# Projecting gates, fox values and memory values 512 columns at a time with four token sums open

## The chip, the cores and the metric

The kernel runs on one core of a Trainium2 chip. The metric is the device time of one execution in microseconds (us); lower is better. A core has a matrix engine (TensorE, "PE" in the profile, with its weight loads listed as PEld), VectorE (DVE), ScalarE (ACT), GpSimd (POOL) and SyncE (SP), which issues most of the transfers. Matrix products accumulate in PSUM, eight banks of 512 float32 columns by 128 partitions.

## What is computed

One layer of a streaming-encoder trunk over 512 tokens of width 1024, in float32:

```python
hn = rmsnorm(h, norm_mix_g[l])
fq, fk, fv, ff, gq, gf, gi, gg = jnp.split(hn @ w_in[l], split_idx, axis=-1)
fox_out = fox_attention(heads(fq), heads(fk), heads(fv), log_f)      # 8 heads of 64, causal, forget bias
rec = hgrn2_chunkwise(gq, gf, gi, lbs[l])                            # 4 heads, gated linear recurrence
rec = rmsnorm(rec, hgrn_norm_g[l]) * silu(gg)
h = h + concat([fox_out, rec]) @ w_out[l]
h = h + memory_cross_attention(rmsnorm(h, norm_x_g[l]), rmsnorm(mem, ...), w_xq[l], w_xkv[l], w_xo[l])
h = h + square(relu(rmsnorm(h, norm_ff_g[l]) @ w1[l])) @ w2[l]
return rmsnorm(h, final_norm_g)
```

Three of these products matter here: the output gates `gg` (512 tokens x 512 columns), the fox values `fv` (512 x 512) and the memory values, the second half of `mem_n @ w_xkv` (256 memory rows x 1024 columns, called xv in the kernel). Each has an inner dimension of 1024.

## The kernel before

**Products.** Every operand is split in two parts, hi (the value rounded to the format float32r) and lo (what the rounding left), and a product is made of three matmuls: hi x hi, hi x lo, lo x hi. The inner dimension is cut into 8 slices of 128 rows. `gemm_fm` makes a block with features on the partitions: 128 weight columns are the stationary operand and 512 tokens move. `gemm_tm` (lines 232 to 243) makes a block with tokens on the partitions: 128 tokens of the activations are stationary and the weight columns move, 256 at a time. The gates, the recurrence's inputs, the fox values and the memory values are made by `gemm_tm`. Two token tiles of 256 columns share one PSUM bank (`proj_tm`, line 547).

**Weights.** `specs` (line 132) lists the weight panels in the order of their use; a panel is 1024 rows by 256 columns. `load_unit` fetches half of it (four row slices, 512 KB) through SyncE's queue into one of two raw buffers; ScalarE then writes the hi part and VectorE the lo part into one of four buffers each. `next_panel` hands out the next panel and keeps one more panel loading ahead.

**PSUM.** The pools are mm (three banks), pv (one), sc (two) and tr (two).

**Order of the work.** The order on TensorE is the order in the code; the other engines' instructions are ordered by a planner by priority. Between the steps of the recurrence and of the fox attention, which wait for VectorE and ScalarE, the code lets TensorE work on projections from a queue called `fill` (class `Fill`, line 249). Each projection is a generator that gives back, after each three matmuls, its cost as a credit: 3n/2400 for n moving columns. `fill.run(us)` adds a credit and takes steps from the queue's head until the credit is used up; `fill.until(name)` takes steps until the named projection is finished, whatever the credit. In order the queue holds: proj_if and gi; the two gate panels (demanded before line 714); proj0, which makes the first pair of fox heads' queries and keys (`fox_proj`); fv0, the first 256 fox value columns; in the fox loop (line 909) proj1 mixed with the transposes of the memory, xv0; proj2, fv256; proj3, xv1 to xv3, and the four memory key panels xk0 to xk3.

**Fox loop.** It runs over 32 units: four pairs of heads, four token blocks, two heads. Unit n's scores are made, then 1.4 of filler (A1), then the output of the block finished three units ago (`fox_out`), then 0.8 of filler (A2), then the transposes of unit n-1's probabilities. At n = 2 the first fox values are demanded (line 931). After the loop what is left of the filler is run, the residual is fetched back (`load_hT`) and the output projection w_out begins (`wo`), whose columns read slices 4 to 7 of the mixed activations (the recurrence) before slices 0 to 3 (the four fox pairs).

**Slots.** Twelve s4 slots of 4 KB per partition hold the recurrence's tensors, the fox values, the memory and its transposes, the memory values and later the residual.

**Lines touched.** 132 to 147 (panels), 172 to 201 (loading), 547 to 583 (gates), 722 to 727 and 895 (fox values), 816 to 827 (memory values), 912 to 931 (the fox loop's demands).

Of the kernel before, what the change touches and what calls it, by code (L numbers as in the profile page):

```python
# [9 lines left out]
F32 = mybir.dt.float32  # L10
R = mybir.dt.float32r
U8 = mybir.dt.uint8
AF = mybir.ActivationFunctionType
# [18 lines left out]
GF = 5  # L32
WARM = 6
P1, P2, P3, P4, PW = 20, 20, 20, 10, -20
MT, NF, V0, LAG = 3, 2, 1, 3
F1, F2, F3, F4, B1 = 1.6, 2.7, 1.5, 1.0, 2.0
A1, A2 = 1.4, 0.8
X1, X2, X3, X4 = 1.5, 2.0, 1.5, 2.0
# [4 lines left out]
def emit(  # L43
# [49 lines left out]
    def s4(shape, name, dt=F32):  # L93
        return s4p.tile([P] + shape, dt, tag="s4", name=name)
# [18 lines left out]
    def mm(name, shape=(S,)):  # L113
        return mmp.tile([P] + list(shape), F32, tag="mm", name=name)

    def pvt(name):
        return pvp.tile([P, S], F32, tag="pv", name=name)
# [7 lines left out]
    def f(a):  # L125
        return a.bitcast(F32)


    def panel(w, n0):
        return [(slice(0, WT), w[:, n0 : n0 + WT].rearrange("(k p) n -> p k n", p=P))]  # L130

    specs = []
    for n0 in (2056, 2312, 1544, 1800, 2568, 2824, 3080, 3336):
        specs.append(panel(w_in, n0))
    specs[4].append((slice(WT, WT + FH), w_in[:, 1536:1544].rearrange("(k p) n -> p k n", p=P)))
    def pair(p):
        return [
            (slice(0, P), w_in[:, p * P : (p + 1) * P].rearrange("(k p) n -> p k n", p=P)),
            (slice(P, 2 * P), w_in[:, 512 + p * P : 512 + (p + 1) * P].rearrange("(k p) n -> p k n", p=P)),
        ]  # L140

    xv = [panel(w_xkv, D + j * WT) for j in range(4)]
    specs += [pair(0), panel(w_in, 1024), pair(1), *xv[0:V0], pair(2), panel(w_in, 1024 + WT), pair(3), *xv[V0:]]
    for j in range(4):
        specs.append(panel(w_xkv, j * WT))
    for w in (w_out, w_xq, w_xo):
# [10 lines left out]
    def new_parts(shape, name):  # L157
        pad = [P, UK * (UW + FH)]
        hi = whp.tile([P, shape[0] * shape[1]], R, tag="wh", name=f"wh{name}", padded_shape=pad)
        lo = wlp.tile([P, shape[0] * shape[1]], R, tag="wl", name=f"wl{name}", padded_shape=pad)  # L160
        return [t.rearrange("p (k n) -> p k n", k=shape[0]) for t in (hi, lo)]
# [10 lines left out]
    def load_unit(name, spec, ks, parts=1, between=None):  # L172

        nw = max(sl.stop for sl, _ in spec)
        hi, lo = new_parts([UK, nw], name)
        raw_ = wrp.tile([P, UK * nw], F32, tag="wr", name=f"wr{name}", padded_shape=[P, UK * UW])
        raw_ = raw_.rearrange("p (k n) -> p k n", k=UK)
        nk = UK // parts
        splits = []
        for q in range(parts):  # L180
            qs, src_ks = slice(q * nk, (q + 1) * nk), slice(ks.start + q * nk, ks.start + (q + 1) * nk)
            for sl, src in spec:
                nc.sync.dma_start(raw_[:, qs, sl], src[:, src_ks, :])
            if between is not None:
                between(q)
            splits.append(split_of(hi[:, qs, :], lo[:, qs, :], raw_[:, qs, :]))
        return (hi, lo), splits

    def load_next(parts=2, between=None):

        i = len(stream)
        if i >= len(specs):
            return []
        units, splits = [], []
        for n in range(2):
            note = None if between is None else (lambda q, n=n: between(n * parts // 2 + q))
            unit, some = load_unit(f"{i}{'ab'[n]}", specs[i], slice(n * UK, (n + 1) * UK), parts // 2, note)
            units.append(unit)
            splits += some
        stream.append(tuple([u[x] for u in units] for x in range(2)))  # L200
        return splits

    def next_panel():
        while len(stream) < min(state["used"] + 2, len(specs)):
            for split in load_next():
                with ahead(PW):
                    split()
        r = stream[state["used"]]
        state["used"] += 1
        return r  # L210
# [21 lines left out]
    def gemm_tm(ps, wt, ahi, alo, tb, nk=KC):  # L232

        whi, wlo = wt
        sl = slice(tb * P, (tb + 1) * P)
        for k in range(nk):
            hi, lo = chunk(ahi, k, sl), chunk(alo, k, sl)
            n = whi[0].shape[2]
            wh, wl = chunk(whi, k, slice(0, n)), chunk(wlo, k, slice(0, n))
            te.matmul(ps, hi, wh, start=k == 0, stop=False)  # L240
            te.matmul(ps, hi, wl, start=False, stop=False)
            te.matmul(ps, lo, wh, start=False, stop=k == nk - 1)
            yield 3 * n / 2400

    def ahead(n):

# [300 lines left out]
    def proj_tm(dst, n0, func, name):  # L547
        wt = next_panel()
        for tp in range(2):
            ps = mm(f"{name}{n0}{tp}", (2, WT))  # L550
            for j in range(2):
                yield from gemm_tm(ps[:, j, :], wt, hn_hi, hn_lo, 2 * tp + j)
            for j in range(2):
                tb = 2 * tp + j
                ac.activation(dst(tb, n0), ps[:, j, :], func, scale=r0[:, tb : tb + 1])

    def rows_of(lst):
        return lambda tb, n0: lst[tb // 2][:, tb % 2, n0 : n0 + WT]

# [19 lines left out]
    fill.add(proj_if(), "ff")  # L579
    fill.add(proj_tm(rows_of(iv), WT, AF.Identity, "gi"))  # L580
    fill.add(new(gg, "gg"))
    for n0 in (0, WT):
        fill.add(proj_tm(rows_of(gg), n0, AF.Silu, "gg"), f"gg{n0}")

# [122 lines left out]

    fill.add(fox_proj(0), "proj0")  # L710

    fill.until("gg256")
    fill.run(F3)
    for hp in range(2):
        pa = tr(f"pa{hp}", (NT, P))
# [3 lines left out]
        fill.run(F4)  # L719


    def new_fv():
        t = s4([NT, WT], f"fv{len(fvt)}")
        fvt.append(t)
        return lambda tb, n0: t[:, tb, :]

    fill.add(proj_tm(new_fv(), 0, AF.Identity, "fv"), "fv0")
    fF = {}

    def fox_rows(p):  # L730
# [83 lines left out]
            yield 0.25  # L814

    def mem_v(j):
        wt = next_panel()
        if j == 0:
            xvh.extend(s4([D], f"xvh{t}", R) for t in range(2))
            xvl.extend(s4([D], f"xvl{t}", R) for t in range(2))  # L820
        ps = mm(f"xv{j}", (2, WT))
        js = slice(j * WT, (j + 1) * WT)
        for t in range(2):
            yield from gemm_tm(ps[:, t, :], wt, me_hi, me_lo, t)
        for t in range(2):
            ac.activation(xvh[t][:, js], ps[:, t, :], AF.Copy)
            ve.tensor_tensor(xvl[t][:, js], ps[:, t, :], f(xvh[t][:, js]), ALU.subtract)

    def mem_k(j):
        wt = next_panel()  # L830
# [54 lines left out]
    def fox_out(p, tb):  # L885
        if tb == 0:
            fpv[p] = pvt(f"pv{p}")
        pv = fpv[p]
        ts_ = slice(tb * P, (tb + 1) * P)
        for sb in range(tb + 1):  # L890
            for j in range(2):
                h = 2 * p + j
                te.matmul(
                    pv[64 * j : 64 * j + 64, ts_],
                    fvt[h // 4][:, sb, h % 4 * FD : (h % 4 + 1) * FD],
                    probT[p, tb, j][:, sb * P : (sb + 1) * P],
                    start=sb == 0,
                    stop=sb == tb,
                )
        if tb == NT - 1:  # L900
            ac.activation(mx_hi[:, p, :], pv, AF.Copy)
            ve.tensor_tensor(mx_lo[:, p, :], pv, f(mx_hi[:, p, :]), ALU.subtract)
# [6 lines left out]
    for n in range(len(units) + LAG):  # L909
        if n < len(units):  # L910
            p, tb, j = units[n]
            if (tb, j) == (0, 0):
                fill.until(f"proj{p}")
                if p == 0:
                    fill.add(zipped(fox_proj(1), mem_T(), ZL), "proj1")
                    for i in range(V0):
                        fill.add(mem_v(i))
                elif p == 1:
                    fill.add(fox_proj(2), "proj2")
                    fill.add(proj_tm(new_fv(), WT, AF.Identity, "fv"), "fv256")  # L920
                elif p == 2:
                    fill.until("fv256")
                    fill.add(fox_proj(3), "proj3")
                    for i in range(V0, 4):
                        fill.add(mem_v(i))
                    for i in range(4):
                        fill.add(mem_k(i))
            if (tb, j) == (3, 0) and p < 3:
                fox_rows(p + 1)
            if n == 2:  # L930
                fill.until("fv0")
            if n + 1 < len(units):
                fox_bias(units[n + 1])
            fox_scores(units[n])
        fill.run(A1)
        if n >= LAG and units[n - LAG][2] == 1:
            fox_out(*units[n - LAG][0:2])
        fill.run(A2)
        if 1 <= n <= len(units):
            fox_T(units[n - 1])  # L940
# [463 lines left out]
```

## Time and profile before

| | |
|---|---|
| median of 3 runs | 786.74 us (785.2 to 787.53) |
| the profiled execution, its own time | 784.74 us |
| its span, first to last instruction | 783.0 us |
| mean granted TensorE clock | 0.998 of full speed |
| HBM read, written | 88.14 MB, 4.21 MB |
| stage of the gates' projection (first and last matmul) | 88.0 to 117.4 us |
| stage of fv0, fv256 | 140.6 to 156, 196.5 to 211 us |
| stage of the memory values | 172 to 181, 227 to 252 us |

How to read it: a row of a view gives the start or the count, the time, the engine, the line of the kernel, the operation, and "out<-in" by the program's names. A name such as wh9a is the hi part of panel 9's first half; hn_hi are the normalised activations; meh and mel the memory's transposes. An arrow "<-" in brackets names the instruction that ended an idle time. Matmuls overlap in a pipeline, so the time of a row is longer than the distance from its start to the next start.

### The profile page before, as it was taken

To read this page: it belongs to the slowest core of one execution; us is meant where nothing else is said; L and a number is where in the kernel's file an instruction comes from. 1 tells how busy PE (TensorE), PEld (TensorE's weight loads), DVE (VectorE), ACT (ScalarE), POOL (GpSimd) and SP (SyncE) were. 2 spreads that over 40 slices of the span, in tenths; PEclk is the share of its full clock that TensorE was granted. 3 is DMA by queue.
4 is the path that set the end of the run, shared out by engine and by line. 5 is a ranking of instruction groups with operands and counts; after the bars stand their busy time and mean duration, and the time that the engine had idled before them with its cause. 6 is when DMAs were issued, how large, how long until landed. Compare 5 with 4: busy or idle time off the path is not lost.

```text
span 783.0 us, 11532 instructions
## 1 busy us (share of the span) xinstructions
PE 770.4 (98%) x4380; PEld 655.1 (84%) x4380; DVE 519.9 (66%) x839; ACT 367.6 (47%) x626; POOL 184.8 (24%) x259
## 2 busy tenths in 40 slices
PE   8999999999999999999999999999999999999996
PEld 5889998978989988888888888888888888888875
DVE  4746755687577656645538646959596877778662
ACT  5655455675565443244434344435353534344433
POOL 7106332414433005410006420100101010100013
PEclk9999999999999999999999999999999999999999
DMA  7543322242443443312222596575748475753302
GB/s 238 193 123 107 98 56 55 82 115 75 162 135 122 148 136 108 107 55 81 70 65 81 179 264 150 155 177 157 183 150 200 136 197 136 194 146 111 77 1 108
DMA packets 80777, 100.43 MB, mean 128 GB/s; under 512 B 4513, under 2 KB 62410, under 8 KB 80722
## 3 DMA queue, kind: packets, MB, share of 16 engines
q1 hardware_dynamic: 72002, 76.08, 30.7%
q0 software_dynamic: 8128, 22.57, 13.5%
q10 hardware_dynamic: 592, 1.05, 0.4%
q8 instruction: 34, 0.56, 0.3%
q14 instruction: 21, 0.17, 0.1%
HBM read 88.14 MB, written 4.21 MB: 118 GB/s over the span
## 4 chain that ended last, share of the span: by engine, by line
PE 96%; DVE 1%; DMA 1%; ACT 1%; issue 0%; POOL 0%; SPq 0%; POOLq 0%
PE u L229 7%; PE u L227 7%; PE u L228 7%; PE U L1280 3%; PE U L1279 3%; PE U L1278 3%; PE xq L227 2%; PE xw L227 2%; PE xw L229 2%; PE xq L229 2%; PE xq L228 2%; PE xw L228 2%; PE wo L227 2%; PE wo L228 2%; PE wo L229 2%; PE Y L1280 2%
## 5 line engine op out<-in xcount | busy, mean ns | idle before, releaser
L168 DVE TENSOR_TENSOR wld<-wq,whd 128x1024 fp32r<-128x1024 f32 x49 | 59.7, 1219 | 24.5 <-ACT whd L166 24.4
L227 PE MATMUL u<-x_hi,whu 128*128 128x512 f32 x192 | 74.7, 389 | 0.0
L228 PE MATMUL u<-x_lo,whu 128*128 128x512 f32 x192 | 74.7, 389 | 0.0
L229 PE MATMUL u<-x_hi,wlu 128*128 128x512 f32 x192 | 74.7, 389 | 0.0
L166 ACT ACTIVATE whd<-wq 128x1024 fp32r<-128x1024 f32 x49 | 51.0, 1051 | 23.7 <-PE u L228 22.1
L166 ACT ACTIVATE whu<-wru 128x1024 fp32r<-128x1024 f32 x24 | 25.3, 1052 | 56.8 <-DMA wru<-in_w_dram 56.8
L168 DVE TENSOR_TENSOR wlu<-wru,whu 128x1024 fp32r<-128x1024 f32 x24 | 29.3, 1220 | 26.4 <-ACT whu L166 26.2
L1156 POOL DMA_DIRECT2D wq<-wq x14 | 12.3, 878 | 136.7 <-DVE wld L168 96.9
L1156 POOL DMA_DIRECT2D wq<-in_w_dram x14 | 17.0, 1217 | 114.4 <-DMA wq<-in_w_dram 99.2
L1278 PE MATMUL U<-whd,hb 128*128 128x512 f32 x112 | 43.6, 389 | 0.0
L1279 PE MATMUL U<-wld,hb 128*128 128x512 f32 x112 | 43.6, 389 | 0.0
L1280 PE MATMUL U<-whd,hb 128*128 128x512 f32 x112 | 43.6, 389 | 0.0
L228 PEld LDWEIGHTS u<-x_lo,whu 128*128 128x128 f32 x192 | 36.0, 188 | 7.5
L227 PEld LDWEIGHTS u<-x_hi,whu 128*128 128x128 f32 x192 | 36.0, 188 | 7.5
L229 PEld LDWEIGHTS u<-x_hi,wlu 128*128 128x128 f32 x192 | 36.0, 188 | 7.4
L1216 ACT ACTIVATE sq<-ur 128x512 f32<-128x512 f32 x32 | 20.0, 626 | 29.1 <-DVE ur L1213 29.1
L1213 DVE SCALAR_TENSOR_TENSOR ur<-u,rbc 128x512 f32<-128x512 f32 x32 | 21.9, 688 | 17.2 <-PE u L229 17.2
L850 POOL TENSOR_SCALAR bi<-nF,Ft 128x128 f32<-128x128 f32 (+3 forms) x32 | 21.3, 664 | 43.0 <-PE pt L877 25.2
L867 ACT ACTIVATE bi<-bi,mx 128x128 f32<-128x128 f32 (+3 forms) x32 | 17.9, 560 | 20.9 <-DVE mx L865 20.6
L1279 PEld LDWEIGHTS U<-wld,hb 128*128 128x128 f32 x112 | 21.0, 188 | 4.4
L1278 PEld LDWEIGHTS U<-whd,hb 128*128 128x128 f32 x112 | 21.0, 188 | 4.4
L1280 PEld LDWEIGHTS U<-whd,hb 128*128 128x128 f32 x112 | 21.0, 188 | 4.3
(950 smaller groups left out, 2452.6 us busy)
## 6 DMA issues: line engine op xcount, KB each, us to landing
wq<-in_w_dram SPq DMA_DIRECT2D x39, 512.0 KB, 3.3
wru<-in_w_dram SPq DMA_DIRECT2D x24, 512.0 KB, 3.8
wq<-in_w_dram POOLq DMA_DIRECT2D x14, 512.0 KB, 8.7
wq<-wq POOLq DMA_DIRECT2D x14, 512.0 KB, 4.6
xTd<-xT POOLq DMA_DIRECT2D x4, 512.0 KB, 3.0
nF<-Fd POOLq DMA_DIRECT2D x8, 256.0 KB, 3.8
hT<-xTd POOLq DMA_DIRECT2D x4, 512.0 KB, 3.5
xt<-in_x_dram SPq DMA_DIRECT2D x3, 512.0 KB
```

The costliest lines, as they stand in the source:

```text
L166: ac.activation(hi, raw, AF.Copy)
L168: ve.tensor_tensor(lo, raw, f(hi), ALU.subtract)
L227: te.matmul(ps, wh, hi, start=n_ == 0, stop=False)
L228: te.matmul(ps, wh, lo, start=False, stop=False)
L229: te.matmul(ps, wl, hi, start=False, stop=n_ == KC - 1)
L850: gp.tensor_scalar(bi[:, 0:n], fF[h][:, 0:n], -1.0, Ft[:, tb, h : h + 1], op0=ALU.mult, op1=ALU.add)
L1156: gp.dma_start(raw.rearrange("p (k n) -> p k n", k=2), src, accum_op=ALU.add)
L1213: ve.scalar_tensor_tensor(u, ps, 0.0, rbc2, op0=ALU.max, op1=ALU.mult)
L1216: ac.activation(sqs[g, j][:, i, :], u, AF.Square)
L1278: te.matmul(ps, hi, whi[:, k, :], start=first_ and k == 0, stop=False, skip_group_check=True)
L1279: te.matmul(ps, hi, wlo[:, k, :], start=False, stop=False, skip_group_check=True)
L1280: te.matmul(ps, lo, whi[:, k, :], start=False, stop=k == 1, skip_group_check=True)
```

## The change

Gates, fox values and memory values are projected 512 columns at a time. A weight panel of these three becomes 512 rows by 512 columns, in two units of 256 rows by 512 columns (`wide`); a unit's size in bytes stays. `gemm_wide` goes through two such panels and keeps one full bank per token tile open: in each unit it does two row slices (six matmuls) for each token tile in turn, and calls `done` for a tile when its last slice is in. For the gates and the fox values the four open banks are the three mm banks and the pv bank; for the memory values two mm banks. The fox values are one projection instead of two, in the layout of the gates, and are demanded whole at unit 2; the fv256 projection inside the fox loop goes. The four memory value panels become two calls, the first in pair 0 and the second in pair 2. The order of the panels follows.

```diff
+    def wide(w, n0):
+        return [[(slice(0, S), w[k0 * P : (k0 + 4) * P, n0 : n0 + S].rearrange("(k p) n -> p k n", p=P))] for k0 in (0, 4)]
...
-    for n0 in (2056, 2312, 1544, 1800, 2568, 2824, 3080, 3336):
+    for n0 in (2056, 2312, 1544, 1800, 2568, 2824):
         specs.append(panel(w_in, n0))
+    specs += wide(w_in, 3080)
...
-    xv = [panel(w_xkv, D + j * WT) for j in range(4)]
-    specs += [pair(0), panel(w_in, 1024), pair(1), *xv[0:V0], pair(2), panel(w_in, 1024 + WT), pair(3), *xv[V0:]]
+    xv = [wide(w_xkv, D + j * S) for j in range(2)]
+    specs += [pair(0), *wide(w_in, 1024), pair(1), *xv[0], pair(2), pair(3), *xv[1]]
...
-        hi, lo = new_parts([UK, nw], name)
+        uk = ks.stop - ks.start
+        hi, lo = new_parts([uk, nw], name)
...
+    def gemm_wide(pss, ahi, alo, done):
+        for half in range(2):
+            whi, wlo = next_panel()
+            for u in range(2):
+                for tb, ps in enumerate(pss):
+                    sl = slice(tb * P, (tb + 1) * P)
+                    for kk in range(2):
+                        k = 4 * half + 2 * u + kk
+                        hi, lo = chunk(ahi, k, sl), chunk(alo, k, sl)
+                        te.matmul(ps, hi, whi[u][:, kk, :], start=k == 0, stop=False)
+                        te.matmul(ps, hi, wlo[u][:, kk, :], start=False, stop=False)
+                        te.matmul(ps, lo, whi[u][:, kk, :], start=False, stop=k == KC - 1)
+                        yield 3 * S / 2400
+                    if k == KC - 1:
+                        done(tb, ps)
...
+    def proj_wide(dst, func, name):
+        pss = [mm(f"{name}{tb}") for tb in range(NT - 1)] + [pvt(f"{name}3")]
+        def done(tb, ps):
+            ac.activation(dst[tb // 2][:, tb % 2, :], ps, func, scale=r0[:, tb : tb + 1])
+        yield from gemm_wide(pss, hn_hi, hn_lo, done)
...
-    for n0 in (0, WT):
-        fill.add(proj_tm(rows_of(gg), n0, AF.Silu, "gg"), f"gg{n0}")
+    fill.add(proj_wide(gg, AF.Silu, "gg"), "gg")
...
-    fill.add(proj_tm(new_fv(), 0, AF.Identity, "fv"), "fv0")
+    fill.add(new(fvt, "fv"))
+    fill.add(proj_wide(fvt, AF.Identity, "fv"), "fv")
...
     def mem_v(j):
-        wt = next_panel()
...
-        ps = mm(f"xv{j}", (2, WT))
-        js = slice(j * WT, (j + 1) * WT)
-        for t in range(2):
-            yield from gemm_tm(ps[:, t, :], wt, me_hi, me_lo, t)
-        for t in range(2):
-            ac.activation(xvh[t][:, js], ps[:, t, :], AF.Copy)
-            ve.tensor_tensor(xvl[t][:, js], ps[:, t, :], f(xvh[t][:, js]), ALU.subtract)
+        js = slice(j * S, (j + 1) * S)
+        def done(t, ps):
+            ac.activation(xvh[t][:, js], ps, AF.Copy)
+            ve.tensor_tensor(xvl[t][:, js], ps, f(xvh[t][:, js]), ALU.subtract)
+        yield from gemm_wide([mm(f"xv{j}{t}") for t in range(2)], me_hi, me_lo, done)
...
-                    fvt[h // 4][:, sb, h % 4 * FD : (h % 4 + 1) * FD],
+                    fvt[sb // 2][:, sb % 2, h * FD : (h + 1) * FD],
...
                 elif p == 1:
                     fill.add(fox_proj(2), "proj2")
-                    fill.add(proj_tm(new_fv(), WT, AF.Identity, "fv"), "fv256")
                 elif p == 2:
-                    fill.until("fv256")
                     fill.add(fox_proj(3), "proj3")
-                    for i in range(V0, 4):
-                        fill.add(mem_v(i))
+                    fill.add(mem_v(1))
...
             if n == 2:
-                fill.until("fv0")
+                fill.until("fv")
```

More of the change, by code (lines that the diff above doesn't have):

```diff
@@ L34 @@
 P1, P2, P3, P4, PW = 20, 20, 20, 10, -20
-MT, NF, V0, LAG = 3, 2, 1, 3
+MT, NF, LAG = 3, 2, 3
 F1, F2, F3, F4, B1 = 1.6, 2.7, 1.5, 1.0, 2.0
@@ L174, in load_unit @@
         nw = max(sl.stop for sl, _ in spec)
-        hi, lo = new_parts([UK, nw], name)
-        raw_ = wrp.tile([P, UK * nw], F32, tag="wr", name=f"wr{name}", padded_shape=[P, UK * UW])
-        raw_ = raw_.rearrange("p (k n) -> p k n", k=UK)
-        nk = UK // parts
+        uk = ks.stop - ks.start
+        hi, lo = new_parts([uk, nw], name)
+        raw_ = wrp.tile([P, uk * nw], F32, tag="wr", name=f"wr{name}", padded_shape=[P, UK * UW])
+        raw_ = raw_.rearrange("p (k n) -> p k n", k=uk)
+        nk = uk // parts
         splits = []
@@ L194, in load_next @@
         units, splits = [], []
+        uk = specs[i][0][1].shape[1] // 2
         for n in range(2):
             note = None if between is None else (lambda q, n=n: between(n * parts // 2 + q))
-            unit, some = load_unit(f"{i}{'ab'[n]}", specs[i], slice(n * UK, (n + 1) * UK), parts // 2, note)
+            unit, some = load_unit(f"{i}{'ab'[n]}", specs[i], slice(n * uk, (n + 1) * uk), parts // 2, note)
             units.append(unit)
@@ L710, in emit @@
     fill.add(fox_proj(0), "proj0")
-    fill.until("gg256")
+    fill.until("gg")
     fill.run(F3)
@@ L719, in emit @@
         fill.run(F4)
[L722 to L725, printed above, removed]
-    fill.add(proj_tm(new_fv(), 0, AF.Identity, "fv"), "fv0")
+    fill.add(new(fvt, "fv"))
+    fill.add(proj_wide(fvt, AF.Identity, "fv"), "fv")
     fF = {}
@@ L915, in emit @@
                     fill.add(zipped(fox_proj(1), mem_T(), ZL), "proj1")
-                    for i in range(V0):
-                        fill.add(mem_v(i))
+                    fill.add(mem_v(0))
                 elif p == 1:
                     fill.add(fox_proj(2), "proj2")
-                    fill.add(proj_tm(new_fv(), WT, AF.Identity, "fv"), "fv256")
                 elif p == 2:
-                    fill.until("fv256")
                     fill.add(fox_proj(3), "proj3")
-                    for i in range(V0, 4):
-                        fill.add(mem_v(i))
+                    fill.add(mem_v(1))
                     for i in range(4):
```

## The prediction

> **What bounds the kernel now.** First the page: span, busy shares, and the shares of the chain that ended last; then TensorE's list of waits.
>
> ```profile
> span 783.0 us, 11532 instructions
> PE 770.4 (98%) x4380; PEld 655.1 (84%) x4380; DVE 519.9 (66%) x839; ACT 367.6 (47%) x626; POOL 184.8 (24%) x259
> PE 96%; DVE 1%; DMA 1%; ACT 1%; issue 0%; POOL 0%; SPq 0%; POOLq 0%
> ```
> ```profile
> PE xn L399 <- DMA xt<-in_x_dram: 1.9, 2, 1.3
> ...
> PE pt L877 <- DVE mel L359: 0.6, 1, 0.6
> PE pa L717 <- DVE A L672: 0.3, 1, 0.3
> ```
>
> TensorE is the chain: 96% of it, with about 13 us of the span idle, most of it at the start and the end. In the stage the change touches (88 to 281 us) the list names two waits, 0.6 and 0.3 us. So a removed matmul cost arrives at the end almost whole, and work taken off VectorE, ScalarE or the queues is worth nothing by itself. "Busy" hides how fast matmuls follow each other, as each row lasts longer than its spacing. The price is therefore read from start times in the order-of-time view: first a stretch of narrow matmuls (fv, 256 columns), then one of wide ones with the operand layout that the change brings (activations as weights, 512 weight columns moving, six matmuls to a bank, then the next bank: the MLP's down product).
>
> ```profile
> 145.79 0.28 PE L240 MATMUL fv<-wh9a,hn_hi 128*128 128x256 f32 x1
> ...
> 149.38 0.28 PE L240 MATMUL fv<-wh9a,hn_hi 128*128 128x256 f32 x1
> ```
> ```profile
> 499.76 0.39 PE L1278 MATMUL U<-whd,hb 128*128 128x512 f32 x1
> ...
> 505.88 0.39 PE L1278 MATMUL U<-whd,hb 128*128 128x512 f32 x1
> ```
>
> Between the two fv rows lie 30 matmuls: 3.59/30 = 0.1197 us from start to start. Between the two U rows lie 27: 6.12/27 = 0.2267 us. Two narrow ones cost 0.2393 us, one wide one 0.2267: 0.0127 us per pair.
>
> **The change, part by part.** *Matmuls merged.* The counts, from the groups of line 240 (one of three product lines; panel halves a and b have a row each):
>
> ```profile
> L240 PE MATMUL gg<-wh6a,hn_hi x16: 283/283/288, 88.0 to 100.1; 128*128 128x256 f32 x16
> L240 PE MATMUL fv<-wh9a,hn_hi x16: 278/283/363, 140.6 to 153.7; 128*128 128x256 f32 x16
> L240 PE MATMUL xv<-wh11a,meh x8: 280/281/364, 172.0 to 178.4; 128*128 128x256 f32 x8
> ```
>
> Gates: 16 x 2 halves x 2 panels x 3 products = 192, fox values 192, memory values 8 x 2 x 4 x 3 = 192: 576 narrow matmuls become 288 wide ones. At 0.0127 us a pair that is 3.65 us, the upper bound. The lower bound comes from wide matmuls that have just followed an interruption by fp32 work:
>
> ```profile
> 117.52 1.06 PE L655 MATMUL lv<-mov,mix 128*128 128x128 f32 x8
> 118.33 0.47 PE L227 MATMUL pq<-hn_hi,wh8a 128*128 128x512 f32 x1
> 118.64 0.39 PE L228 MATMUL pq<-hn_lo,wh8a 128*128 128x512 f32 x1
> ...
> 120.26 0.39 PE L229 MATMUL pq<-hn_hi,wl8a 128*128 128x512 f32 x1
> ```
>
> Seven spacings in 1.62 us are 0.2314 each; a pair then saves 0.2393 - 0.2314 = 0.0079, and 288 of them 2.3 us. The projections are filler, interrupted every 6 to 15 matmuls, but some 60 of them run in long stretches. I take 3.2 us, nearer the steady rows, since U has exactly the new form and only the first half dozen spacings of a run are slow.
>
> [...]
>
> *Interruptions.* A filler run still gives way once per call, since every credit of 0.8 or more buys at least one step of 0.64. Does a wide neighbour make the interruption dearer? A wide and a narrow run around the same 12 pv matmuls:
>
> ```profile
> 181.99 0.39 PE L229 MATMUL pq<-hn_hi,wl12a 128*128 128x512 f32 x1
> 182.31 0.88 PE L893 MATMUL pv<-pts,fv 128*64 128x128 f32 x12
> ...
> 183.45 0.39 PE L228 MATMUL pq<-hn_lo,wh12a 128*128 128x512 f32 x1
> ```
> ```profile
> 240.92 0.28 PE L242 MATMUL xv<-wh16a,mel 128*128 128x256 f32 x1
> 241.13 0.88 PE L893 MATMUL pv<-pts,fv 128*64 128x128 f32 x12
> ...
> 242.16 0.28 PE L241 MATMUL xv<-wl16b,meh 128*128 128x256 f32 x1
> ```
>
> From the last matmul before to the second after: 1.46 - 2 x 0.2267 = 1.01 us wide, 1.24 - 2 x 0.1197 = 1.00 us narrow. Nothing lost or won.
>
> *Filler moved.* Counted through the code's credits (a wide step 0.64, a narrow one 0.32): before, the demand for fv0 at unit 2 forces no step; 10 narrow fv steps are forced at the start of pair 2, and 13 of xk3 are left after the fox loop. Now all of fv must be done at unit 2, so 11 wide steps are forced there (33 x 0.2267 = 7.5 us), 2 of proj2 at pair 2, and nothing is left behind the loop. Forced steps are useful TensorE work, so the total is unchanged; two places need a look. At unit 2, this is what waited there:
>
> ```profile
> 160.57 0.33 PE L877 MATMUL pt<-ident,bi 128*128 128x128 f32 x1 [0.57 <-DVE mel L359]
> 153.90:180.90 27.00, 26.43 (x174) 22.48 (x173) 21.27 (x55) 20.02 (x42) 7.42 (x17) 1.00 0.35 98
> ```
>
> The transpose of unit 1 waited 0.57 us on VectorE, which is 21.27 of 27.0 us busy in pair 0 (fourth value of the stage row, 79%). The forced 7.5 us stand before that transpose now and cover it: up to -0.6. But the memory transposes and proj1 then start two units later and meet larger units: the same VectorE work, minus the xv evacuations, in fewer units, worth up to +1.5 (a rival below). I take zero for both. At the loop's end, w_out's first column has 21 matmuls (4.8 us) before it reads the last pair's values:
>
> ```profile
> 275.38 1.09 PE L893 MATMUL pv<-pts,fv 128*64 128x128 f32 x16
> 276.52 0.60 ACT L901 ACTIVATE mx_hi<-pv 128x512 fp32r<-128x512 f32 x1
> 277.90 0.68 DVE L902 TENSOR_TENSOR mx_lo<-pv,mx_hi 128x512 fp32r<-128x512 f32 x1
> 281.64 1.23 DVE L168 TENSOR_TENSOR wl23a<-wr23a,wh23a 128x1024 fp32r<-128x1024 f32 x1 [3.06 <-ACT wh23a L166]
> 281.91 0.40 PE L227 MATMUL wo<-mx_hi,wh22b 128*128 128x512 f32 x1
> ```
>
> pv ends at 276.47 and mx_lo at 278.58: 2.1 us. The 13 xk3 steps that covered it are gone, but 4.8 us remain; one weight split ahead of it (1.23) still fits, two leave it about even. Zero, at worst +0.5.
>
> *Banks and queues.* Four sums are open at once: three mm banks and pv. For fv the third mm bank is the one pk0 leaves; VectorE empties it late:
>
> ```profile
> L703 DVE TENSOR_TENSOR ks<-pk,rbc x4: 674/684/691, 143.5 to 227.1; 128x512 f32<-128x512 f32 x4
> 145.35 0.36 PE L240 MATMUL fv<-wh9b,hn_hi 128*128 128x256 f32 x1
> 149.49 1.13 DVE L781 SCALAR_TENSOR_TENSOR rec<-po,hr,gg 128x128 f32<-128x128 f32 x4 [2.58 <-POOL hr L339]
> ```
>
> ks is done at 144.2. The third token tile begins with the fifth wide step, behind the transposes of chunk 2, where the 145.35 row stands, some 0.2 us later as 4 x 0.68 us replace 7 x 0.36: a slack of 1.3 us. Zero. pv was last read long before, and fv's part of it is emptied units before the first fox output needs it.
>
> *Evacuations, loads, moved tiles.* Evacuations halve in number and double in width, on engines with idle time:
>
> ```profile
> L555 ACT ACTIVATE gg<-gg,r x8: 465/470/473, 97.9 to 118.1; 128x256 f32<-128x256 f32 x8
> L827 DVE TENSOR_TENSOR xvl<-xv,xvh x8: 403/418/425, 182.2 to 255.0; 128x256 fp32r<-128x256 f32 x8
> ```
>
> Zero; uncovered, each gate evacuation would cost under 1 us, but its bank is not wanted by proj0 until the last six matmuls (1.4 us) and a level later. Weight units keep 512 KB, two per panel, at the same spacing in matmul time (48 x 0.2267 = 10.9 us a unit pair, 96 x 0.1197 = 11.5 before), with half as many rows to fetch, on SyncE's queue alone. Both fox value tiles are live early: with the memory tiles that makes 12 of 12 s4 slots, none short; two of the late residual loads on POOL's queue must wait for the last fox output; w_out needs them from its fifth column on, after 4 x 24 x 0.2267 = 21.8 us. Zero.
>
> **Sum.** The profiled execution took 784.74 us: less 3.2 makes 781.5. The median of the runs shown is 2.0 above that execution, so on its scale 786.74 - 3.2 = 783.5 us.
>
> **The rivals.** *The pair price is small.* If every wide matmul stays in the slow spacing after an interruption and the pair-0 pass gives back 0.5, 2.3 - 0.5 = 1.8 us are left: 784.9. For it: the 0.2314 rows in this very stage. Against: U, and the long forced stretch. [...]
>
> *VectorE becomes the bound in pair 0.* 79% busy on the mean, and squeezed: three or four transposes waiting 0.5 us as at 160.57 give back 1.5 to 2 us: 785.2. Against: its xv subtractions (2 x 0.42 us) leave that pass, and 7.5 us of forced matmuls let its queue drain first.
>
> *A bank comes late* (slower). ks is queued behind the last chunk's rec, which waits for POOL and ends at 150.6: then ks ends at 151.3 and TensorE, in order, stands from 145.6 to 151.3 before fv's third tile: 5.7 us, less the gain 2.5 us slower, 789.2. It decides once ks ends after 145.6, and costs the whole gain at 148.8. For it: ScalarE and VectorE are ordered by a planner, which may reorder. Against: ks is emitted before chunk 3 and stood at 143.5.
>
> *The filler runs dry before the loop's end*: by the credits it ends in the last call; one fox round without cover would cost about 1 us. Within the range.
>
> **How the numbers follow.** Forecast 0.62 (2.4 to 4.4 us of gain, so 782.3 to 784.3); small pair price 0.13 (784.9); VectorE 0.12 (785.2); late bank or another new wait of that size 0.09 (789.2); gains beyond the sum, such as the wait at 160.57 gone too, 0.04 (781.5). A measurement here tells from no change about 0.3%, 2.4 us. Faster by more: the forecast, the larger gain and a little of the next two, 0.68; within: 0.22; slower: 0.10. The three runs shown spread by 2.3 us, so the range reaches a little beyond the cases: 780.8 to 786.6.
>
> **What would show it.** Right: wide gg, fv and xv rows spaced 0.227 in long stretches and up to 0.232 after interruptions, 288 matmul instructions fewer, no new TensorE wait above 0.5 us between 88 and 290 us, the start of w_out near 278.5 instead of 281.9. Wrong: spacing of 0.239 or a longer run-in; waits before fv at the third tile, before pt in pair 0, or before the first w_out column.

## The result and the profile after

The forecast was 783.5 us, a gain of 3.2. The changed kernel takes 788.83 us, the median of 22 runs (785.95 to 791.03); the kernel before, run beside it, 784.74 (22 runs, 783.8 to 787.53). The ratio is 1.0044, with an interval of 1.0034 to 1.0054: slower by 0.3 to 0.5%, with the medians 4.1 us apart, and outside the range of 780.8 to 786.6. The profiled execution took 786.98 us. First its page, in the lines that answer to those of before, and below them TensorE's list of waits (engine, line, tile waited for; total, times, longest).

```profile
span 785.0 us, 10933 instructions
...
PE 770.1 (98%) x4092; PEld 639.6 (81%) x4092; DVE 519.2 (66%) x835; ACT 366.1 (47%) x614; POOL 186.2 (24%) x259
...
PE 93%; DVE 2%; DMA 1%; ACT 1%; POOL 1%; issue 1%; SPq 0%; POOLq 0%; ACTq 0%
```
```profile
PE ps L885 <- ACT kh L738: 3.2, 2, 2.1
...
PE ps L886 <- DVE kl L739: 0.6, 2, 0.3
PE rbc L1377 <- POOL r L363: 0.4, 1, 0.4
PE pr L781 <- DVE rec L808: 0.4, 1, 0.4
PE lv L686 <- issue: 0.3, 1, 0.3
```

The 288 instructions are gone (4380 to 4092), and so are the two waits that stood in this stage before (pt on mel, pa on A). Two small ones have come, lv (0.3) and pr on rec (0.4), and two larger ones at places that the prediction did not look at, though they break its general sign (no new wait above 0.5 us): the first score matmuls of a pair of heads (ps, lines 885 and 886) wait for ScalarE's and VectorE's copies of that pair's keys, kh and kl. This table is worked out from the first starts of gg, proj0's pq, fv and wo in the traces (us):

| kernel | gg to proj0 | proj0 to fv | fv to w_out | sum | w_out to the last matmul |
|---|---|---|---|---|---|
| before | 30.33 | 22.30 | 141.28 | 193.91 | 493.76 |
| after | 29.93 | 21.76 | 144.07 | 195.77 | 494.55 |

The first two stages gained 0.9 us. The fox loop, which should have gained most, lost 2.8. Here is where, in order of time (start, duration, engine, line); first pair 2's start, then pair 1's.

```profile
214.06 0.60 PE L903 MATMUL pt<-ident,bi 128*128 128x128 f32 x4
...
214.41 0.48 PE L234 MATMUL pk<-hn_hi,wh14b 128*128 128x512 f32 x1
...
215.65 0.40 PE L236 MATMUL pk<-hn_hi,wl14b 128*128 128x512 f32 x1
215.85 1.06 ACT L171 ACTIVATE wh16b<-wr16b 128x1024 fp32r<-128x1024 f32 x1 [0.50 <-PE pk L235]
216.09 0.69 DVE L734 TENSOR_TENSOR ks<-pk,rbc 128x512 f32<-128x512 f32 x1 [0.50 <-PE pk L236]
216.81 0.63 ACT L737 ACTIVATE kh<-ks 64x512 fp32r<-64x512 f32 x1
...
217.47 0.63 ACT L738 ACTIVATE kh<-ks 64x512 fp32r<-64x512 f32 x1
...
218.15 0.33 PE L885 MATMUL ps<-kh,q 128*128 128x128 f32 x1 [2.10 <-ACT kh L738]
...
218.81 0.33 PE L886 MATMUL ps<-kl,q 128*128 128x128 f32 x1 [0.34 <-DVE kl L739]
```
```profile
182.63 0.40 PE L236 MATMUL pk<-hn_hi,wl11b 128*128 128x512 f32 x1
...
183.01 0.48 PE L262 MATMUL xv<-wh12a,meh 128*128 128x512 f32 x1
...
183.08 0.69 DVE L734 TENSOR_TENSOR ks<-pk,rbc 128x512 f32<-128x512 f32 x1
...
183.80 0.71 ACT L893 ACTIVATE bi<-bi,mx 128x512 f32<-128x512 f32 x1
...
184.25 0.39 PE L264 MATMUL xv<-wh12a,mel 128*128 128x512 f32 x1
...
184.48 0.60 PE L903 MATMUL pt<-ident,bi 128*128 128x128 f32 x4
184.50 0.45 ACT L382 ACTIVATE meh<-mnt,gv 128x256 fp32r<-128x256 f32 x1
184.86 0.62 ACT L737 ACTIVATE kh<-ks 64x512 fp32r<-64x512 f32 x1
...
185.50 0.63 ACT L738 ACTIVATE kh<-ks 64x512 fp32r<-64x512 f32 x1
...
186.18 0.33 PE L885 MATMUL ps<-kh,q 128*128 128x128 f32 x1 [1.10 <-ACT kh L738]
...
186.74 0.33 PE L886 MATMUL ps<-kl,q 128*128 128x128 f32 x1 [0.23 <-DVE kl L739]
```

At pair 2 the last key matmul of proj2 starts at 215.65 and the next thing in TensorE's order is the score that reads those keys. From one to the other run a scaling (0.69), two copies (0.63 each) and the subtraction: TensorE stands for most of 218.15 - 215.65 = 2.50 us and then 0.66 more. At pair 1 six matmuls of xv0 (183.01 to 184.25) and a few transposes lie between, and 1.10 + 0.23 us are left. ScalarE is part of this one: ks is done at 183.77, but ScalarE first works on bi and meh, and kh begins at 184.86. In the kernel before, the same distance at pair 2 was 15.6 us, filled with fv256:

```profile
195.79 0.40 PE L229 MATMUL pk<-hn_hi,wl12b 128*128 128x512 f32 x1
...
211.43 0.22 PE L859 MATMUL ps<-kh,q 128*128 128x128 f32 x1
```

### The profile page after: what moved, and what is told of

Its sections match the earlier page's. It is cut to its first block, busy times and chain, and to the rows that moved or that the text cites. A ratio compares the mean times of both kernels' runs of the same rounds, so it can differ in the third digit from the quotient of the medians.

```text
span 785.0 us, 10933 instructions
## 1 busy us (share of the span) xinstructions
PE 770.1 (98%) x4092; PEld 639.6 (81%) x4092; DVE 519.2 (66%) x835; ACT 366.1 (47%) x614; POOL 186.2 (24%) x259
## 4 chain that ended last, share of the span: by engine, by line
PE 93%; DVE 2%; DMA 1%; ACT 1%; POOL 1%; issue 1%; SPq 0%; POOLq 0%; ACTq 0%
PE u L236 7%; PE u L234 7%; PE u L235 7%; PE U L1302 3%; PE U L1300 3%; PE U L1301 3%; PE xq L234 2%; PE wo L234 2%; PE xw L234 2%; PE xw L236 2%; PE xq L236 2%; PE xq L235 2%; PE xw L235 2%; PE wo L236 2%; PE wo L235 2%; PE Y L1302 2%
```

## The experiments

Three theories were set against each other at first. *Order* (called late keys below): the loss comes from the order of the filler, which lets proj1 and proj2 end where their keys are first read. *Overload* (rival A): VectorE and ScalarE have too much to do in that stage, wherever the projections stand. *Width* (rival B): the loss comes from the wide matmuls themselves, by four open banks, larger bursts or a run-in after each interruption. The table of stages for all kernels (us) comes first, with the short reports below.

| kernel | gg to w_out | fv to w_out | time, us (runs) | ratio to before, interval |
|---|---|---|---|---|
| before | 193.91 | 141.28 | 784.74 (22) | |
| after | 195.77 | 144.07 | 788.83 (22) | 1.0044 [1.0034, 1.0054] |
| proj2_first | 196.05 | 144.35 | 788.14 (6) | 1.0037 [1.0025, 1.0049] |
| narrow_new_order | 200.13 | 147.50 | 791.73 (6) | 1.0088 [1.0071, 1.0104] |
| gates_wide_only | 193.02 | 141.31 | 784.25 (12) | 0.9993 [0.9983, 1.0002] |
| projs_first | 200.99 | 149.27 | 794.25 (4) | 1.0112 [1.0097, 1.0127] |
| fv_narrow | 192.26 | 140.55 | 783.53 (7) | 0.9973 [0.9963, 0.9984] |
| fv_before_loop | 191.78 | 140.07 | 784.11 (9) | 0.9979 [0.9968, 0.999] |
| wide_no_key_wait | 191.09 | 139.37 | 783.66 (8) | 0.9968 [0.9953, 0.9982] |
| narrow_no_key_wait | 193.47 | 140.83 | 785.45 (12) | 0.9995 [0.9986, 1.0004] |

The first four experiments shared one set of runs of the kernel before (median 784.99), the next four another (786.14); each ratio is against its own set.

**Narrow, in the new order.** The kernel before, 256 columns wide everywhere, but with both fv panels queued and demanded at unit 2, so that fv256 inside the fox loop goes, and with two memory value panels in front of proj2 instead of one (V0).

```diff
-MT, NF, V0, LAG = 3, 2, 1, 3
+MT, NF, V0, LAG = 3, 2, 2, 3
...
-    specs += [pair(0), panel(w_in, 1024), pair(1), *xv[0:V0], pair(2), panel(w_in, 1024 + WT), pair(3), *xv[V0:]]
+    specs += [pair(0), panel(w_in, 1024), panel(w_in, 1024 + WT), pair(1), *xv[0:V0], pair(2), pair(3), *xv[V0:]]
...
-    fill.add(proj_tm(new_fv(), 0, AF.Identity, "fv"), "fv0")
+    for n0 in (0, WT):
+        fill.add(proj_tm(new_fv(), n0, AF.Identity, "fv"), f"fv{n0}")
...
-                fill.until("fv0")
+                fill.until("fv256")
```

> The kernel before with its narrow matmuls, but with the filler's order of the changed kernel: both fox value panels in front of proj1 and demanded whole at unit 2, two memory value panels between proj1 and proj2, the other two behind proj3. Theory (the order costs, the width does not): waits for kh at pairs 1 and 2 of about 4 us in all, 784.74 + 4 = 788.7 us, slower than the changed kernel by the gain of the merged matmuls. Rival B (the width costs): no such waits, 784 to 785.5 us.

Slower still, by 0.7 to 1.0%, with the same two waits and no wide projection in it:

```profile
PE ps L860 <- ACT kh L707: 3.5, 2, 2.1
...
PE ps L861 <- DVE kl L708: 0.6, 2, 0.3
```

So the order costs without any wide matmul. It is also 3 us over the 788.7 expected. Part of that is a second loss, taken up below: its trace (200.13) has the clock at half from 222.61 to 226.02, right behind the gap at pair 2.

**Only the gates wide**; fox values and memory values as before.

```diff
-    for n0 in (2056, 2312, 1544, 1800, 2568, 2824, 3080, 3336):
+    for n0 in (2056, 2312, 1544, 1800, 2568, 2824):
...
+    specs += wide(w_in, 3080)
...
-    for n0 in (0, WT):
-        fill.add(proj_tm(rows_of(gg), n0, AF.Silu, "gg"), f"gg{n0}")
+    fill.add(proj_wide(gg, AF.Silu, "gg"), "gg")
```

> The kernel before with only the gates projected 512 columns at a time; fox values and memory values stay narrow, the filler's order in the fox loop stays. Theory: 96 pairs at 0.004 to 0.0127 us, so 0.4 to 1.2 us less than before: 783.5 to 784.3 us, no new wait above 0.5 us. Rival B (the width costs): 785 us or more.

No wait for kh. The gates' stage is 0.4 us shorter as in the changed kernel, and by w_out the trace has gained 0.9; the total cannot be told from no change.

**proj2 ahead of the memory values.** The changed kernel, with xv0 moved behind proj2, so that proj2 ends earlier.

```diff
-    specs += [pair(0), *wide(w_in, 1024), pair(1), *xv[0], pair(2), pair(3), *xv[1]]
+    specs += [pair(0), *wide(w_in, 1024), pair(1), pair(2), *xv[0], pair(3), *xv[1]]
...
-                    fill.add(mem_v(0))
                 elif p == 1:
                     fill.add(fox_proj(2), "proj2")
+                    fill.add(mem_v(0))
```

> The changed kernel with one edit: in pair 1 of the fox loop the queries and keys of pair 2 (proj2) are projected before the memory values xv0, no longer after them; pair 1 keeps its order. Theory (late keys: proj2 now ends in the very call in which pair 2 needs it, so TensorE stands while ScalarE and VectorE make kh and kl): the wait of the score matmuls at the start of pair 2, 2.5 + 0.67 us from start to start, goes; the one at pair 1, 1.38 + 0.56 us, stays; profiled time 786.98 - 2.7 = 784.3 us. Rival A (the scores wait because VectorE and ScalarE are overloaded in that stage, wherever proj2 stands): the wait stays or moves, 786 to 787 us. Rival B (wide matmuls themselves are what is dearer): no change, 787 us.

A miss: 788.14 instead of about 784.3, and what rival A had written, "the wait stays or moves", is nearer. The wait at pair 2 is gone, but the one at pair 1 has grown, because the two steps of xv0 that stood between proj1's end and pair 1 in the changed kernel were its cover. ScalarE adds to it again: ks is done at 185.08, and kh begins at 186.65, behind bi, meh and pts.

```profile
183.95 0.39 PE L236 MATMUL pk<-hn_hi,wl11b 128*128 128x512 f32 x1
184.18 0.38 PE L380 MATMUL mnt<-ident,mt 128*128 128x128 f32 x2
184.40 0.60 PE L903 MATMUL pt<-ident,bi 128*128 128x128 f32 x4
187.98 0.33 PE L885 MATMUL ps<-kh,q 128*128 128x128 f32 x1 [2.98 <-ACT kh L738]
```

And it showed something that the waits do not hold: what follows the gap is slow. The stretches behind it (times of PE, PEld, DVE, ACT, POOL with counts; then the granted clock, DMA share, GB/s):

```profile
187.00:188.00 1.00, 0.02 (x1) 0.02 (x1) 1.00 (x3) 0.95 (x3) 0.00 (x0) 1.00 0.12 37
188.00:189.00 1.00, 1.00 (x3) 0.88 (x4) 0.55 (x2) 0.97 (x2) 0.00 (x0) 0.59 0.85 254
189.00:190.00 1.00, 1.00 (x4) 0.78 (x3) 0.60 (x3) 0.56 (x3) 0.00 (x0) 0.50 0.61 234
190.00:191.00 1.00, 1.00 (x4) 0.81 (x3) 0.45 (x2) 0.16 (x2) 0.00 (x0) 0.50 0.00 0
191.00:192.00 1.00, 1.00 (x4) 0.59 (x3) 0.00 (x0) 0.00 (x0) 0.00 (x0) 0.71 0.00 0
192.00:193.00 1.00, 1.00 (x14) 0.68 (x13) 0.00 (x0) 0.00 (x0) 0.00 (x0) 1.00 0.00 0
```

**Projections ahead of everything.** As the last one, and proj1 not mixed with the memory transposes but ahead of them.

```diff
-                    fill.add(zipped(fox_proj(1), mem_T(), ZL), "proj1")
-                    fill.add(mem_v(0))
+                    fill.add(fox_proj(1), "proj1")
+                    fill.add(mem_T())
```

> The same edit for both pairs: proj2 before xv0, and in pair 0 the 16 steps of proj1 all before the transposes of the memory, no longer mixed with them. Theory (late keys): both waits go; 786.98 - 4.3 = 782.7 us in the profiled run, under the kernel before, and no execution near 790 us if the long waits are also what lowers the granted clock in some executions. Rival A (overload): memory transposes in a lump make new waits of 1 us or more each, 785 to 787 us. Rival B: 787 us.

The worst of all, 794.25 instead of 782.7. No score waits for kh any more, but the transposes of the memory, in one lump, wait for VectorE, as rival A had it:

```profile
PE mnt L380 <- DVE mel L383: 4.6, 2, 3.9
...
PE pt L903 <- DVE mel L383: 1.3, 2, 0.7
```

The clock is at half behind the first of these waits, from 186.98 to 197.22. The mixing of proj1 with the transposes is a cover too. Whoever moves one projection in this queue moves the cover of another.

**The price of the key waits, wide and narrow.** To take the waits away without moving anything, the first token block of pairs 1 and 2 reads the queries and keys of the pair before; what these kernels compute for that block is therefore other scores. The same edit stands once in the changed kernel and once in the narrow one in the new order.

```diff
-        kh, kl = fk[p]
+        o = p - 1 if p in (1, 2) and tb == 0 else p
+        kh, kl = fk[o]
...
-        te.matmul(ps[:, 0:n], fq[p][j][:, ts_], kh[:, j, 0:n], start=True, stop=False)
+        te.matmul(ps[:, 0:n], fq[o][j][:, ts_], kh[:, j, 0:n], start=True, stop=False)
```

> The changed kernel, but the scores of the first token block of pairs 1 and 2 (two units each) are made from the queries and keys of the pair before; everything is still projected and split. So no score waits for keys that were just made. Theory (late keys are the loss, and their idle time lowers the granted clock in some executions): 786.98 - 4.3 = 782.7 us in the profiled run, clock 0.998 in every execution, all of them within 1.5 us of each other. Rival (wide matmuls or the busier VectorE are dearer by themselves): 786 us or more.

> The narrow matmuls in the changed kernel's order, with the same replacement of the keys in the first token block of pairs 1 and 2. It differs from the run wide_no_key_wait by the width alone. Theory: 288 pairs at 0.0079 to 0.0127 us, so 2.3 to 3.65 us slower than that run, about 785 to 786 us, near the kernel before. [...]

This pair gives both terms. From gg to w_out the waits cost 195.77 - 191.09 = 4.7 us in the changed kernel. The width, in one and the same order and without the waits, gains 193.47 - 191.09 = 2.4 us, or 0.0083 a pair of narrow matmuls; by the medians of the runs it is 785.45 - 783.66 = 1.8 us. The wide kernel without the waits is faster than before by 0.2 to 0.5%; the narrow one cannot be told from it. Two forecasts for the wide one failed: its runs have clocks of 0.996 to 0.998, not 0.998 throughout, and spread over 3.8 us, not 1.5. Its trace has the full clock from 20 to 770 us, so the spread has another source than the waits, which is not known. The time ahead of the first gg matmul alone, which this edit does not touch, is 89.8 us in its trace and 87.4 in the changed kernel's.

**Two ways to give the cover back.** First, the fox values narrow again in two halves at the old places, gates and memory values wide:

```diff
-    specs += [pair(0), *wide(w_in, 1024), pair(1), *xv[0], pair(2), pair(3), *xv[1]]
+    specs += [pair(0), panel(w_in, 1024), pair(1), *xv[0], pair(2), panel(w_in, 1024 + WT), pair(3), *xv[1]]
...
                     fill.add(fox_proj(2), "proj2")
+                    fill.add(proj_tm(new_fv(), WT, AF.Identity, "fv"), "fv256")
```

> The changed kernel with the fox values as before: two narrow panels, the first demanded at unit 2, the second between proj2 and pair 2. Gates and memory values stay 512 columns wide. Theory (proj1 and proj2 ended just in time for their pairs because all of fv was forced ahead of them): proj1 starts at unit 0 again and proj2 has filler behind it, both waits go, 192 pairs save 1.5 to 2.4 us: 782.5 to 783.5 us, under the kernel before. Rival A (overload of VectorE by the wide evacuations): waits stay, 786 us.

Second, all wide, with the demand for fv moved from unit 2 to just before the fox loop, one line:

```diff
+    fill.until("fv")
     for n in range(len(units) + LAG):
...
-            if n == 2:
-                fill.until("fv")
```

> The changed kernel with all of fv demanded before the fox loop and not at unit 2: the same forced work, two units earlier, so that proj1 starts at unit 0 as before. Theory: the wait at pair 1 goes (1.6 us) and that at pair 2 shrinks, as proj2 ends one call or more before pair 2; but the filler is dry some 4.7 credits before the loop's end, where the last units then wait for VectorE and ScalarE, 1 to 3 us: 783 to 787 us. Rival A: waits at both pairs stay, 787 us or more.

Both beat both kernels: 0.9973 [0.9963, 0.9984] and 0.9979 [0.9968, 0.999]. With the second, proj1 and proj2 end earlier by the credit of the units that now don't pay for fv, and what is left of the key waits is one row:

```profile
PE ps L885 <- ACT kh L738: 0.6, 1, 0.6
```

The penalty expected of it, filler running dry before the loop's end, did not show: the list has no wait there, and its stage is 191.78, against 195.77 in the changed kernel and 191.09 without the key waits. It also speaks against the overload as the main cause: all evacuations are as wide as in the changed kernel, and the waits for kh are down from 3.2 us to 0.6.

**The clock behind a gap.** The changed kernel's 22 runs fall apart by their mean granted clock:

| mean granted clock | runs | time, us |
|---|---|---|
| 0.997 to 0.998 | 8 | 785.95 to 787.65 |
| 0.992 to 0.996 | 14 | 787.99 to 791.03 |

The mean alone does not tell where the clock fell. The kernel before has 0.995 or 0.996 in 6 of the 17 runs of its first set, and they average 785.3 us against 785.1 of the others; fv_narrow and fv_before_loop were traced at 0.996, and there the clock is at half for 3.4 us between 7.5 and 11.8 us, far ahead of the stages compared here. The profiled execution (786.98) belongs to the faster eight, so the changed kernel was profiled twice more.

> The changed kernel once more, unchanged, to see in a trace what its runs at a lower mean granted clock (0.992 to 0.996, 788 to 791 us) do. If the clock theory is right, a profiled run with a mean clock of 0.996 or less shows a window of 3 to 4 us right behind one of the two key waits (at about 186 or 218 us) in which the granted clock is near one half and the wide matmuls start 0.43 us apart instead of 0.227, which costs some 1.5 to 2 us, and the rest of the execution is spaced as before; a run at 0.997 or above shows no such window. If instead the lower mean clock comes from somewhere else (the start, the cross attention, the MLP), the windows behind the key waits stay at 1.00 in both.

> The same kernel and the same question, since 14 of 22 runs had the lower clock and one look may miss it: a window of about half the clock right behind a key wait if the mean is 0.996 or less, none if it is 0.997 or more.

The first of the two ran at 0.998 (786.38 us, 195.76 from gg to w_out), with the clock at 1.00 behind both gaps. The second ran at 0.996 (788.1 us, 197.21). Its gap at pair 2 is the same 2.49 us, and behind it the clock falls to half (windows; columns as above; the six from 220.8 to 223.8 all show 0.50):

```profile
219.80:220.30 0.50, 0.50 (x4) 0.42 (x3) 0.28 (x2) 0.18 (x1) 0.00 (x0) 1.00 0.71 229
220.30:220.80 0.50, 0.50 (x3) 0.41 (x2) 0.15 (x1) 0.31 (x2) 0.00 (x0) 0.66 0.96 328
220.80:221.30 0.50, 0.50 (x3) 0.36 (x2) 0.29 (x2) 0.00 (x0) 0.00 (x0) 0.50 0.89 340
...
223.30:223.80 0.50, 0.50 (x7) 0.17 (x3) 0.00 (x0) 0.00 (x0) 0.00 (x0) 0.50 0.00 0
223.80:224.30 0.50, 0.50 (x3) 0.46 (x3) 0.00 (x0) 0.00 (x0) 0.38 (x1) 0.93 0.00 0
```
```profile
219.25 0.45 PE L234 MATMUL pq<-hn_hi,wh15a 128*128 128x512 f32 x1
...
220.84 0.63 PE L234 MATMUL pq<-hn_hi,wh15a 128*128 128x512 f32 x1
221.27 0.63 PE L235 MATMUL pq<-hn_lo,wh15a 128*128 128x512 f32 x1
221.70 0.63 PE L236 MATMUL pq<-hn_hi,wl15a 128*128 128x512 f32 x1
```

The first row is where the filler goes on behind the gap; in the lower three the matmuls start 0.43 us apart instead of 0.227. That one spell accounts for the whole difference of the two executions in this stage: 197.21 - 195.76 = 1.45 us.

## Why the prediction was wrong

**The step that failed is "Filler moved".** It counted the steps rightly: demanding all of fv at unit 2 forced 33 wide matmuls there (157.66 to 165.04 in the rows further below), and two steps of proj2, six matmuls, were forced at the start of pair 2 (214.41 to 215.65). From this it concluded: "Forced steps are useful TensorE work, so the total is unchanged; two places need a look." It looked at unit 2 and at the loop's end. The third place was in its own sentence: proj2 ends at the start of pair 2, and the instruction behind it reads what proj2 makes. A forced matmul is worth its time only if something independent covers the way from its result to its reader, here ks, two copies and kl. By the rows TensorE stands 2.10 + 0.34 us for it at pair 2 and 1.10 + 0.23 at pair 1, 3.8 in all; the experiment without the waits puts the whole loss at 4.7 us (what makes up the rest was not itemised), more than the forecast gain. The changed kernel, proj2_first and narrow_new_order all pay for that way, wide or narrow.

**The clock was not foreseen.** The 14 runs with the lower mean clock average 789.5 us, the other eight 786.7; the one execution of this kind that was traced loses 1.45 us to a half-clock spell. It goes with the waits: between 20 and 770 us, the half-clock spells of all twelve traces stand behind such gaps, and the kernel before has neither (1.00 over those 750 us). The rest of the 2.8 us is open: a full spell of 3.41 us with a matmul every 0.43 instead of 0.227 us costs 1.6 (an estimate), and behind the gap at pair 1 (187 to 195 us) the clock is 1.00 in all three traced executions of the changed kernel.

**Matmuls merged: mechanism right, size too large.** In the forced stretch at unit 2 the wide rows go as the upper bound has it once they have run in:

```profile
157.66 0.47 PE L262 MATMUL fv<-wh10a,hn_hi 128*128 128x512 f32 x1
...
159.83 0.39 PE L262 MATMUL fv<-wh10b,hn_hi 128*128 128x512 f32 x1
...
164.59 0.39 PE L262 MATMUL fv<-wh10b,hn_hi 128*128 128x512 f32 x1
...
165.04 0.39 PE L264 MATMUL fv<-wh10b,hn_lo 128*128 128x512 f32 x1
```

From 159.83 to 164.59 there are 21 spacings in 4.76 us, 0.2267 each. But over all 288 pairs the gain was 2.4 us, 0.0083 a pair, which is close to the lower bound (2.3, 0.0079), not the 3.2 taken. The lower bound's rows, wide matmuls behind an interruption, were nearer: between neighbours of these projections, without the key waits, 498 of 545 narrow spacings are within 3.5 ns of 0.1197, but only 133 of 259 wide ones within 3.5 ns of 0.2267. Their means, 0.1233 and 0.2377, leave 2 x 0.1233 - 0.2377 = 0.0089 a pair.

**The sum by what was measured.** The order without the waits, wide, stands 193.91 - 191.09 = 2.8 us below before: 2.4 for the width and 193.91 - 193.47 = 0.4 for the order, in which pt's wait on mel is gone. (The 2.4 are what is left after small waits: with the width pa's 0.3 went, and lv's 0.3 and pr's 0.4 came.) The waits take 4.7. That leaves +1.9 us to w_out (195.77 against 193.91) and 0.8 behind it in the profiled execution (494.55 against 493.76). Of these, 0.6 arise at the wait for r (rbc): the second and third execution don't have that wait and take 493.92 there, while fv_narrow and narrow_no_key_wait have it, so it comes and goes. Ahead of gg the profiled execution was 0.6 us shorter (87.4 against 88.0). 1.9 + 0.8 - 0.6 = 2.1 is what the spans show, 785.0 against 783.0. The eight runs at the higher clock stand 786.7 - 784.7 = 2.0 us above the kernel before; the other 14 carry the median on to 4.1. The forecast's scale was off as well: it stood on the median of three runs, 786.74, and 22 runs have 784.74, so that a gain of 3.2 would have meant 781.5.

**The rivals.** *Late bank*: its time, 789.2, is nearly the result, but its mechanism did not occur; no fv waits at its third tile. The 0.09 given to it and "another new wait of that size" was too little for a change that moves a demand. *VectorE the bound in pair 0*: the contrary; it is 63% busy there, and pt no longer waits. What delays kh at pair 1 is ScalarE's queue, as shown above.

```profile
152.00:180.00 28.00, 27.96 (x142) 22.31 (x142) 17.75 (x44) 16.82 (x34) 7.71 (x13) 1.00 0.29 94
```

*Small pair price*: partly true, as above. *Filler dry*: no such wait in the list. **Right otherwise**: the chain stays on TensorE, the weights keep up (no new DMA wait), no wait names the wide evacuations, and the wait at 160.57 is covered by the forced stretch. The start of w_out was expected 3.4 us earlier (near 278.5 instead of 281.9). Counted from the first gg matmul, because the time ahead of it varies, it came 1.9 us later, and without the key waits 2.8 us earlier.

## What to carry to other kernels

When a change moves the point up to which filler work must be done, write down for each producer in that queue the distance from its last instruction to its first reader, and what independent work lies in it, before and after: where it shrinks below the way through the other engines (here 2.5 us at pair 2, and 3.6 at pair 1, where ScalarE had other work first), the difference is paid, though the sum of the work has not changed. Cover is borrowed: reordering one projection uncovered another twice in these runs, and the cheap cure was to move the demand, not the work.

## What the runs showed of the hardware

A short standstill of TensorE cost more than its length in four of the traces. Behind gaps of 2.49 us from start to start (the changed kernel's third execution and narrow_new_order), 3.25 us (proj2_first) and 4.2 us (projs_first) the granted clock fell to 0.50. From the windows above the spell of the changed kernel lasted 0.34 + 3.0 + 0.07 = 3.41 us, the one of proj2_first 0.41/0.5 + 2 + 0.29/0.5 = 3.4 us; the one of narrow_new_order, 222.61 to 226.02, lasted 3.41 us, and that of projs_first three times as long, 10.24 us. In the changed kernel it began only after work had resumed, 1.2 us after (from 219.25 to 220.80 - 0.34 = 220.46), and the same gap brought none in two other executions.

In the 3.41 us ahead of the fall the rows show TensorE busy for these shares:

| trace | stretch ahead of the fall, us | busy share |
|---|---|---|
| changed kernel, third execution | 217.05 to 220.46 | 0.50 |
| narrow_new_order | 219.20 to 222.61 | 0.28 |
| proj2_first | 184.76 to 188.18 | 0.13 |
| projs_first | 183.56 to 186.98 | 0.00 |

In the changed kernel's first execution the stretch that lies in the same way about the gap, 216.78 to 220.19, has 0.50 too, and the clock stayed at 1.00 (218.8 to 227). So neither the gap's length nor this share tells which execution of the changed kernel loses the clock; what does is not shown here. These are few traces; that 14 of 22 runs had the lower mean clock says how often, not where.
